# Three pairs of column groups of each feed-forward computed by Strassen's seven block products

## The chip, the cores and the metric

The kernel runs on one core of one Trainium2 chip. The metric is the device time of one execution in microseconds (us). A core has a matrix engine (TensorE; PE in the rows, its weight loads PEld), a vector engine (VectorE; DVE), a scalar engine (ScalarE; ACT), a general one (GpSimd; POOL) and a queue that issues transfers (SP). Each engine works through its own list of instructions in order, and semaphores hold an instruction until what it reads is there. TensorE writes into PSUM banks of 128 x 512 numbers; the other engines take the numbers from there to the on-chip buffer SBUF.

## The reference

256 tokens of width 1024 go through four layers, two of a first kind and two of a second. Each layer is a feed-forward, a mixer and another feed-forward, with norms between them. So there are eight feed-forwards, and all of them are

```
a, b = split(x @ w13, 2, axis=-1)      # x [256, 1024], w13 [1024, 2 x 2816]
(silu(a) * b) @ w2                     # w2 [2816, 1024]
```

In the second kind of layer x is the output of an RMS norm. Everything is float32.

## The kernel before

**Numbers.** TensorE multiplies in a format that keeps fewer bits than float32 (fp32r). Every operand is therefore split into a high part (a rounded copy, made by ScalarE) and a low part (operand minus high part, made by VectorE), and every product is made of three: high x high, high x low, low x high (`mm3`, L245).

**Weights.** They come as a stream of 712 units of 128 x 1024 numbers (512 KB). `fetch` (L197) loads a unit into one of four staging buffers `stg` through the SP queue; `split` (L205) makes `wh` (L215, ScalarE) and `wl` (L221, VectorE, a few on GpSimd) in two halves of 512 columns, so 4 instructions a unit. The split tiles lie in a ring of 48 buffers of 128 x 512, which is 12 units. A buffer is free again when the last matmul that reads it is done.

**Tokens.** The 256 tokens are two tiles of 128, each a generator (`tokens`). The second one lags by some units. The program is written in the order in which the generators are called; `split` is called some units ahead of the first tile (`lead`, L186). A scheduler then fixes the order on TensorE, ScalarE and VectorE at build time by priority and by what is ready and has a buffer; SP and GpSimd keep the order of the program.

**A feed-forward** (`ffn`, L324) has 11 groups of 256 columns of a and the same 256 of b.
- Groups 0 and 1: each tile by itself (`group`, L259), x as the stationary operand and 512 columns of weights streamed past it; then `hidden` and a transpose of the result (`transposed`, L230).
- Groups 2 to 10: both tiles together (`joint`, L363). The weights are stationary and the 256 tokens are streamed (L375), which gives the transposed result at once. A unit takes 24 matmuls of 256 columns; a group has four units. `gate` (L397) takes silu(a) b and splits it.
- Between the groups, `joint` multiplies what is finished with w2 (L387, by `mm3`), a unit of w2 at a time, with 12 matmuls of 512 columns for both tiles. The order is groups 2-3, 8 units of w2, groups 4-7, 8 units of w2, groups 8-10; the last 6 units of w2 each tile takes by itself (`rows`, L274).

Before a feed-forward the norm's result is transposed by TensorE and split into `xh` and `xl` (`to_x`, L251; ScalarE at L256, VectorE at L257).

Of the kernel before, what the change touches and what calls it, by code (L numbers as in the profile page):

```python
# [19 lines left out]
P = 128  # L20
# [10 lines left out]
# units by which the second token tile lags, and by which weights are split ahead; units in the  # L31
# ring of split weights, of which the last TAIL of a product are held longer; loads in flight
# [6 lines left out]
TAIL = 2  # L39
LAGS = dict(ffn=9, mixer1=6, mixer2=6)  # L40
# [3 lines left out]
# ticks between the steps of work that runs beside the products  # L44
# [23 lines left out]
class Core:  # L68
    """The two tiles of 128 tokens go through the network as two generators. Each yields after
    every unit of weights (one tick) it has multiplied with, or a number of ticks to be left  # L70
    alone; the second one lags, so that what lies between the products of one tile runs beside
    products of the other. Every engine issues in the order of this program."""

    def __init__(self, ctx, tc, a, out, order):
# [5 lines left out]
        self.whp = p("whp", 4 * RING)  # L80
# [5 lines left out]
        self.nunit = a["ws"].shape[0]  # L86
        self.phase = []
        for what, _ in order:
            for kind, n in (("ffn", 66), ("mixer1", 56) if what == "b1" else ("mixer2", 36), ("ffn", 66)):
                self.phase += [(kind, m) for m in range(n)]  # L90
# [30 lines left out]
    def start(self, g):  # L121
        """A generator of work beside the products; it yields ticks to wait."""
        done = {"done": False}

        def go():
            n = next(g, None)
            if n is None:
                done["done"] = True
            else:
                self.later(n, go)  # L130

        go()
        return done
# [5 lines left out]
    def run_all(self):  # L139
# [3 lines left out]
        def part(i, h):  # L143
            hi, lo = (t[:, i, 512 * h:512 * h + 512] for t in (self.xh, self.xl))
# [20 lines left out]
        while any(live):  # L165
# [20 lines left out]
    def lead(self):  # L186
        """Weights are split further ahead where the first tile is in a norm or the second one
        soon will be."""
        kind, n = self.phase[min(self.pos[0], self.nunit - 1)]
        left = dict(ffn=66, mixer1=56, mixer2=36)[kind] - n  # L190
        return LEAD + (MORE if n < FIRST else max(0, MORE - left // RAMP))

# [4 lines left out]
    def fetch(self, v):  # L197
        while self.next_dma <= min(v, self.nunit - 1):
            t = self.stg.tile([P, 1024], F32, tag="stg", name=self.nm("stg"))
            for c in (slice(0, 512), slice(512, 1024)) if self.next_dma == 0 else (slice(0, 1024),):  # L200
                self.nc.sync.dma_start(t[:, c], self.a["ws"][self.next_dma][:, c])
            self.stages[self.next_dma] = t
            self.next_dma += 1

    def split(self, u):  # L205
        while self.next_split <= min(u, self.nunit - 1):
            v = self.next_split
            self.fetch(v)
            w = self.stages.pop(v)
            wh, wl = [], []  # L210
            for h in range(2):
                half = w[:, h * 512:h * 512 + 512]
                wh.append(self.whp.tile([P, 512], F32R, tag="w", name=self.nm("wh")))
                wl.append(self.whp.tile([P, 512], F32R, tag="w", name=self.nm("wl")))
                r = self.nc.scalar.activation(wh[h], half, AF.Copy)  # L215
                if v < 3:
                    self.pin(r)
                if h and self.pool_share(*self.phase[v]):
                    self.nc.gpsimd.tensor_tensor(wl[h], half, wh[h], op=ALU.subtract)
                else:  # L220
                    self.nc.vector.tensor_sub(wl[h], half, wh[h])  # L221
            self.units[v] = (wh, wl)
# [13 lines left out]
    def to_T(self, src, name="xT"):  # L236
        """[tokens, 512] -> the two parts of its transpose [128, 4, tokens]."""
# [7 lines left out]
    def mm3(self, accs, xh, xl, wh, wl, start, stop):  # L245
        """accs[c] += x^T w[:, c] in the three products of parts that matter in float32."""
# [12 lines left out]
    def group(self, i, fn, extra=None):  # L259
        """A group of 512 columns, in units of two k-tiles."""  # L260
# [31 lines left out]

    def part(self, *xT):
# [5 lines left out]
    def row(self, src):  # L299
        """A row of 512, in every partition."""  # L300
# [8 lines left out]
    def prepare(self, i, n, *what):  # L309
        """Rows that both tiles use some time later, loaded once."""  # L310
# [1124 lines left out]
```

## Time and profile before

| | |
|---|---|
| time, median of 3 runs | 2220.77 us (2216.96 to 2222.27) |
| the profiled execution, from its first to its last instruction (span) | 2218.5 us |
| TensorE busy | 2184.9 us, 98% |
| VectorE busy | 1486.9 us, 67% |
| ScalarE busy | 1185.5 us, 53% |
| GpSimd busy | 282.5 us, 13% |
| mean transfer rate | 178 GB/s |

The page of the profile gives no other time of the profiled execution than its span; the median of the runs is 2.3 us more. Matmuls are pipelined, so their busy times overlap: what one costs is read from start to start, not from its duration.

### The profile page before, as it was taken

To read this page: it belongs to the slowest core of one execution; us is meant where nothing else is said; L and a number is where in the kernel's file an instruction comes from. 1 tells how busy PE (TensorE), PEld (TensorE's weight loads), DVE (VectorE), ACT (ScalarE), POOL (GpSimd) and SP (SyncE) were. 2 spreads that over 40 slices of the span, in tenths; PEclk is the share of its full clock that TensorE was granted. 3 is DMA by queue.
4 is the path that set the end of the run, shared out by engine and by line. 5 is a ranking of instruction groups with operands and counts; after the bars stand their busy time and mean duration, and the time that the engine had idled before them with its cause. 6 is when DMAs were issued, how large, how long until landed. Compare 5 with 4: busy or idle time off the path is not lost.

```text
span 2218.5 us, 35915 instructions
## 1 busy us (share of the span) xinstructions
PE 2184.9 (98%) x13440; PEld 1948.5 (88%) x13440; DVE 1486.9 (67%) x2553; ACT 1185.5 (53%) x2203; POOL 282.5 (13%) x319
## 2 busy tenths in 40 slices
PE   8999999999999999999999999999999999999998
PEld 7998888899899888889989997788998998788998
DVE  5656787655755779775585668776658566787463
ACT  5644755554544475554453554755446355576452
POOL 0000420000000033001001005610100100650000
PEclk9999999999999999999999999999999999999999
DMA  7854455655555445565545633527555464244561
GB/s 265 271 186 160 146 188 172 232 186 188 186 200 186 156 157 183 187 205 197 199 159 183 226 135 113 186 87 246 188 183 177 163 231 147 96 153 160 173 219 48
DMA packets 115327, 395.03 MB, mean 178 GB/s; under 512 B 12880, under 2 KB 15312, under 8 KB 115152
## 3 DMA queue, kind: packets, MB, share of 16 engines
q1 hardware_dynamic: 115152, 392.73, 52.1%
q8 instruction: 105, 1.72, 0.3%
q14 instruction: 70, 0.57, 0.1%
HBM read 391.63 MB, written 1.05 MB: 177 GB/s over the span
## 4 chain that ended last, share of the span: by engine, by line
PE 92%; DVE 4%; ACT 2%; DMA 1%; issue 1%; POOL 1%; SPq 0%; DVEq 0%; POOLq 0%; ACTq 0%
PE g L375 37%; PE big L249 27%; PE g L249 21%; PE g L233 2%; DMA stg<-in_ws_dram 1%; DVE wl L221 1%; PE big L1130 1%; PE big L660 1%; PE big L1159 1%; DVE qk L1001 1%; ACT wh L215 0%; PE big L1077 0%; PE big L862 0%; ACT xh L256 0%; PE big L1049 0%
## 5 line engine op out<-in xcount | busy, mean ns | idle before, releaser
L221 DVE TENSOR_TENSOR wl<-stg,wh 128x512 fp32r<-128x512 f32 x1410 | 966.1, 709 | 483.5 <-ACT wh L215 444.2
L215 ACT ACTIVATE wh<-stg 128x512 fp32r<-128x512 f32 x1424 | 846.9, 626 | 582.8 <-PE g L375 237.7
L375 PE MATMUL g<-xh,wh 128*128 128x256 f32 x2304 | 652.6, 283 | 0.0
L375 PE MATMUL g<-xl,wh 128*128 128x256 f32 x2304 | 652.0, 283 | 0.0
L375 PE MATMUL g<-xh,wl 128*128 128x256 f32 x2304 | 652.0, 283 | 0.0
L375 PEld LDWEIGHTS g<-xh,wl 128*128 128x128 f32 x2304 | 442.2, 192 | 0.9
L375 PEld LDWEIGHTS g<-xh,wh 128*128 128x128 f32 x2304 | 442.2, 192 | 0.9
L375 PEld LDWEIGHTS g<-xl,wh 128*128 128x128 f32 x2304 | 442.2, 192 | 0.0
L249 PE MATMUL g<-wh,xh 128*128 128x512 f32 x800 | 330.2, 413 | 11.2 <-ACT wh L215 6.7
L249 PE MATMUL g<-wl,xh 128*128 128x512 f32 x800 | 316.4, 396 | 0.0
L249 PE MATMUL g<-wh,xl 128*128 128x512 f32 x800 | 315.7, 397 | 0.5 <-DVE xl L257 0.3
L249 PEld LDWEIGHTS g<-wh,xh 128*128 128x128 f32 x800 | 152.8, 191 | 44.3 <-ACT wh L215 7.4
L249 PEld LDWEIGHTS g<-wh,xl 128*128 128x128 f32 x800 | 152.3, 190 | 36.8 <-DVE xl L257 3.9
L249 PE MATMUL big<-wh,hTh 128*128 128x512 f32 x576 | 182.8, 389 | 0.0
L249 PE MATMUL big<-wh,hTl 128*128 128x512 f32 x576 | 182.6, 389 | 0.0
L249 PE MATMUL big<-wl,hTh 128*128 128x512 f32 x576 | 182.6, 389 | 0.0
L249 PEld LDWEIGHTS g<-wl,xh 128*128 128x128 f32 x800 | 152.8, 191 | 27.6 <-DVE wl L221 0.4
L321 POOL TENSOR_TENSOR m<-m,nhalf 128x1 f32<-128x1 f32 (+1 forms) x24 | 23.1, 962 | 852.7 <-DVE m L320 852.7
L249 PEld LDWEIGHTS big<-wl,hTh 128*128 128x128 f32 x576 | 108.1, 188 | 22.6
L249 PEld LDWEIGHTS big<-wh,hTl 128*128 128x128 f32 x576 | 108.1, 188 | 22.5
L249 PEld LDWEIGHTS big<-wh,hTh 128*128 128x128 f32 x576 | 107.1, 188 | 21.3
L484 POOL TENSOR_TENSOR m<-m,nhalf 128x1 f32<-128x1 f32 x24 | 15.3, 638 | 646.6 <-DVE m L483 646.6
(297 smaller groups left out, 2158.9 us busy)
## 6 DMA issues: line engine op xcount, KB each, us to landing
stg<-in_ws_dram SPq DMA_DIRECT2D x711, 512.0 KB, 4.2
row<-in_norm_gain_dram SPq DMA_DIRECT2D x24, 256.0 KB, 5.6
row<-in_ln_g_dram SPq DMA_DIRECT2D x12, 256.0 KB, 4.8
row<-in_ln_b_dram SPq DMA_DIRECT2D x12, 256.0 KB, 6.3
xT<-in_xT_dram SPq DMA_DIRECT2D x4, 256.0 KB, 6.0
x<-in_x_dram SPq DMA_DIRECT2D x4, 256.0 KB, 6.9
out_dram<-x SPq DMA_DIRECT2D x4, 256.0 KB, 2.0
con<-in_con_dram SPq DMA_DIRECT2D x1, 528.0 KB, 6.9
```

Of the source, the lines that this page charges most:

```text
L215: r = self.nc.scalar.activation(wh[h], half, AF.Copy)
L221: self.nc.vector.tensor_sub(wl[h], half, wh[h])
L233: self.nc.tensor.transpose(tp[:, hs(j)], src[:, hs(j)], self.ident)
L249: self.nc.tensor.matmul(accs[c], a, b[c], start=start and q == 0, stop=stop and q == 2)
L321: self.nc.gpsimd.tensor_tensor(out, out, self.nhalf[:, 0:n], op=ALU.pow)
L375: nc.tensor.matmul(out, w[k // 4][:, hs(k % 4)], x[:, :, hs(k)], start=k + q == 0, stop=k == 7 and q == 2)
L484: self.nc.gpsimd.tensor_tensor(rs, rs, self.nhalf[:, 0:1], op=ALU.pow)
L660: nc.tensor.matmul(ps[:, 64 * h:64 * h + 64].rearrange("p (c m) -> p c m", m=m), Z[:, hs(h)], view(Z[:, hs(h)], m)[:, :, 1, :], start=True ...
L1001: eng.scalar_tensor_tensor(t[:, to], src[:, at], w(j), t[:, to], op0=ALU.mult, op1=ALU.add)
L1130: nc.tensor.matmul(ps[:, hh * S + j * P:hh * S + j * P + P], J["aq", i][r, hs(head // 2)], J["ak", j][r, hs(head // 2)], start=True, stop= ...
L1159: nc.tensor.matmul(o[:, 64 * hh:64 * hh + 64], pT[:, hs(2 * hh + j)], J["av", j][:, head * 64:head * 64 + 64], start=j == 0, stop=j == 1)
```

## The change

Of the nine groups that both tiles take together, six (2-3, 4-5, 6-7) are now done as three pairs. For a pair, x is a 2 x 2 matrix of blocks (two tiles of 128 tokens by two halves of 512 of the width; A11 to A22) and the weights are one too (two halves of the width by 512 columns of a and 512 of b; 11 to 22). Instead of eight block products, seven are made (`PRODUCTS`), each 128 tokens x 512 x 512 columns, as two units.

- `sums`: once a feed-forward, four sums of blocks of x (VectorE) and their splits. For that `to_x` keeps an unsplit copy of the transposed x where a feed-forward follows (`keep`).
- `operand`: the weight blocks are loaded unsplit into the ring (`raw`); four of the seven products need a sum of blocks, which VectorE makes, two units each, over 1024 columns.
- `split` of such a unit is one ScalarE and one VectorE instruction over 1024 columns instead of two of 512 each. The ring has the same size, but in 24 buffers of 128 x 1024, and now also holds the raw blocks and the sums.
- `pair`: the matmuls have x (or a sum) stationary and 512 columns of weights streamed. Several products add up in the same bank; ScalarE copies the intermediate states out of it (`keep`), VectorE adds them. The result lies by tokens and is transposed (`to_T`), 8 transposes of 128 x 128 a pair.
- The order is: pair 2-3, four units of w2, group 8, pair 4-5, four of w2, group 9, two of w2, pair 6-7, four of w2, group 10, two of w2; then the last six of w2. `lead` is 5 units where a pair is near.

Comments are also taken out. The number of loaded bytes is the same. Core of the diff:

```diff
+PAIR = 5
...
-BLOCKS = ((0, 4), (4, 8), (8, 11))
+FFN = (("s", 2), ("r", 0, 4), ("j", 8), ("s", 4), ("r", 4, 8), ("j", 9), ("r", 16, 18), ("s", 6),
+       ("r", 8, 12), ("j", 10), ("r", 18, 20))
+LAST = (12, 13, 14, 15, 20, 21)
+
+PRODUCTS = ("p1", "q5", "p6", "p3", "p7", "p2", "q4")
+NEEDS = dict(p1="11", q5="12", p6="22", p2="21")
...
-        self.whp = p("whp", 4 * RING)
+        self.whp = p("whp", 2 * RING)
...
-                self.split(min(self.pos[0] + self.lead(), self.next_split + STEP - 1))
+                self.split(min(self.pos[0] + self.lead(), self.next_split + STEP - 1 + self.paired()))
...
+        if self.made[min(self.pos[0] + PAIR, self.nunit - 1)]:
+            return PAIR
...
+    def operand(self, p, u):
+        raw, add = self.raw, self.nc.vector.tensor_add
+        if p == "p1":
+            return raw["11", u]
+        if p == "q5":
+            t = raw.pop(("11", u))
+            add(t, t, raw["12", u])
+            raw["t1", u] = t
+            return t
+        if p == "p6":
+            t = raw["t2", u] = self.whp.tile([P, 1024], F32, tag="w", name=self.nm("sum"))
+            add(t, raw.pop(("t1", u)), raw["22", u])
+            return t
+        if p == "p3":
+            return raw["22", u]
+        if p == "p7":
+            t = raw.pop(("12", u))
+            add(t, t, raw.pop(("22", u)))
+            return t
+        if p == "p2":
+            return raw["21", u]
+        t = raw.pop(("t2", u))
+        add(t, t, raw.pop(("21", u)))
+        return t
...
+            for h, c in enumerate(halves if made is None else [slice(0, 1024)]):
+                r = self.nc.scalar.activation(hi[:, c], w[:, c], AF.Copy)
...
+                    self.nc.vector.tensor_sub(lo[:, c], w[:, c], hi[:, c])
...
-    def to_x(self, i, srcs):
+    def to_x(self, i, srcs, keep=False):
...
+            if keep:
+                t = self.sh["A", i, h] = self.slot(name="A")
+                self.nc.scalar.activation(t, tp, AF.Copy)
...
+    def sums(self):
+        nc = self.nc
+        a11, a12, a21, a22 = (self.sh.pop(("A", i, h)) for i in range(2) for h in range(2))
+        nc.vector.tensor_sub(a22, a22, a21)
+        nc.vector.tensor_sub(a21, a11, a21)
+        nc.vector.scalar_tensor_tensor(a11, a22, -1.0, a11, op0=ALU.mult, op1=ALU.subtract)
+        nc.vector.scalar_tensor_tensor(a12, a11, -1.0, a12, op0=ALU.mult, op1=ALU.subtract)
+        X = {}
+        for p, t in (("q5", a22), ("p6", a11), ("p3", a12), ("p7", a21)):
+            hi, lo = self.slot((P, 512), F32R, "Xh"), self.slot((P, 512), F32R, "Xl")
+            nc.scalar.activation(hi, t, AF.Copy)
+            nc.vector.tensor_sub(lo, t, hi)
+            X[p] = hi, lo
+        for p, i, h in (("p1", 0, 0), ("p2", 0, 1), ("q4", 1, 1)):
+            X[p] = tuple(t[:, i, 512 * h:512 * h + 512] for t in (self.xh, self.xl))
+        return X
...
+    def pair(self, J, g):
+        nc = self.nc
+        bank, kept = {}, {}
+
+        def keep(p):
+            t = kept[p] = self.slot(name="k" + p)
+            nc.scalar.activation(t, bank[p], AF.Copy)
...
+        def hidden(i, t, sg):
+            nc.vector.scalar_tensor_tensor(t, t, -0.5 if J["rs", i] is None else -1.0, sg,
+                                           op0=ALU.mult, op1=ALU.mult)
+
+            def turn():
+                hi, lo = self.to_T(t, "hT")
+                for c in range(4):
+                    J["h", i, 2 * g + c] = hi[:, hs(c)], lo[:, hs(c)]
+
+            self.later(2, turn)
+
+        for p in PRODUCTS:
+            if p in ("p1", "q5", "p2"):
+                bank[p] = self.bank(self.grp, "g")
+            else:
+                bank[p] = bank["q5" if p == "p3" else "p1"]
+            xh, xl = J["X"][p]
+            for u in range(2):
                 wh, wl = self.units[self.pos[1]]
+                for j in range(2):
+                    k = 2 * u + j
+                    for q, (x, w) in enumerate(((xh, wh), (xh, wl), (xl, wh))):
+                        nc.tensor.matmul(bank[p], x[:, hs(k)], w[j], start=p in ("p1", "q5", "p2") and k + q == 0,
+                                         stop=k == 3 and q == 2, skip_group_check=True)
...
+                if u:
+                    if p in ("p1", "q5", "p6", "p7"):
+                        keep(p)
+                    if p == "p3":
+                        t = kept["p6"]
+                        nc.vector.tensor_add(t, t, bank[p])
+                    elif p == "p7":
+                        t = kept["p7"]
+                        nc.vector.tensor_add(t, t, kept.pop("q5"))
+                    elif p == "p2":
+                        t = kept.pop("p1")
+                        nc.vector.tensor_add(t, t, bank[p])
+                        silu(t, t, 0)
+                        hidden(0, kept.pop("p6"), t)
+                    elif p == "q4":
+                        t = self.slot(name="sg")
+                        silu(t, bank[p], 1)
+                        hidden(1, kept.pop("p7"), t)
                 yield
```

## Rows read from the trace of the kernel before

**Rows 1.** The page: busy time, share of the span, instructions; granted clock in 40 slices.
```profile
PE 2184.9 (98%) x13440; PEld 1948.5 (88%) x13440; DVE 1486.9 (67%) x2553; ACT 1185.5 (53%) x2203; POOL 282.5 (13%) x319
...
PEclk9999999999999999999999999999999999999999
```

**Rows 2.** The chain that ended last, in order of time: start, length, what.
```profile
60.02 21.79 PE big L249 x96
81.81 46.07 PE g L375 x384
...
211.30 19.06 PE g L249 x84
```

**Rows 3.** The same chain, transposes of one norm's result, 205 to 230 us.
```profile
210.43 0.87 PE g L233 x8
```

**Rows 4.** Busy time of each engine in the eight joint stages: last stage, then sum.
```profile
2047.50:2195.00 147.50, 147.50 (x1060) 139.97 (x1059) 79.01 (x124) 66.30 (x114) 0.00 (x0) 1.00 0.49 168
sum 1179.20, PE 1179.13 PEld 1118.38 DVE 679.72 ACT 586.28 POOL 34.74; mean PE 147.39 PEld 139.80 DVE 84.96 ACT 73.29 POOL 4.34
```

**Rows 5.** Groups by line, shapes apart: line, engine, operation, shapes | busy us, mean ns.
```profile
L411 DVE TENSOR_TENSOR hTl<-sg,hTh 128x512 fp32r<-128x512 f32 x72 | 49.8, 691 | 13.6 <-ACT hTh L410 9.7
...
L347 DVE TENSOR_TENSOR hT<-g,hT 128x256 fp32r<-128x256 f32 x32 | 13.4, 419 | 2.7 <-ACT hT L346 2.5
...
L256 ACT ACTIVATE xh<-g 128x512 fp32r<-128x512 f32 x44 | 23.8, 595 | 28.0 <-PE g L233 27.9
...
L346 ACT ACTIVATE hT<-g 128x256 fp32r<-128x256 f32 x32 | 12.1, 377 | 14.4 <-PE g L233 10.5 <-issue 3.6
```

**Rows 6.** Timeline of VectorE from 99 us.
```profile
99.16 3.17 DVE L221 TENSOR_TENSOR wl<-stg,wh 128x512 fp32r<-128x512 f32 x5
102.54 0.69 DVE L221 TENSOR_TENSOR wl<-stg,wh 128x512 fp32r<-128x512 f32 x1 [0.22 <-ACT wh L215]
103.98 0.69 DVE L221 TENSOR_TENSOR wl<-stg,wh 128x512 fp32r<-128x512 f32 x1 [0.75 <-ACT wh L215]
```

**Rows 7.** Timeline of ScalarE from 99 us.
```profile
99.46 1.14 ACT L215 ACTIVATE wh<-stg 128x512 fp32r<-128x512 f32 x2
...
103.32 0.63 ACT L215 ACTIVATE wh<-stg 128x512 fp32r<-128x512 f32 x1 [0.81 <-PE g L375]
```

**Rows 8.** Line 215 from 0 to 407.6 us, then from 0 to 596.8 us.
```profile
L215 ACT ACTIVATE wh<-stg x282: 612/631/659, 5.1 to 406.7; 128x512 fp32r<-128x512 f32 x141
...
L215 ACT ACTIVATE wh<-stg x415: 612/631/659, 5.1 to 596.5; 128x512 fp32r<-128x512 f32 x139
```

**Rows 9.** Waits, the longest in total: engine, line, releaser, us in total, times.
```profile
DVE wl L221 <- ACT wh L215: 444.2, 481, 4.8
ACT wh L215 <- PE g L375: 237.7, 310, 1.2
```

**Rows 10.** Busy time in the 24 us ahead of each joint stage: one, then sum.
```profile
573.00:597.00 24.00, 24.00 (x112) 19.56 (x113) 21.21 (x38) 15.17 (x29) 0.99 (x1) 1.00 0.53 182
...
sum 192.00, PE 188.01 PEld 152.66 DVE 167.58 ACT 131.81 POOL 10.82; mean PE 23.50 PEld 19.08 DVE 20.95 ACT 16.48 POOL 1.35
```

**Rows 11.** Timeline of VectorE, 570 to 583 us, first and last of 19 rows.
```profile
570.40 0.68 DVE L221 TENSOR_TENSOR wl<-stg,wh 128x512 fp32r<-128x512 f32 x1
...
582.18 0.42 DVE L347 TENSOR_TENSOR hT<-g,hT 128x256 fp32r<-128x256 f32 x1
```

**Rows 12.** Timeline of TensorE after one norm, 200 us.
```profile
200.41 1.03 PE L233 MATMUL g<-con,x 128*128 128x128 f32 x8
201.70 0.50 PE L249 MATMUL g<-wh,xh 128*128 128x512 f32 x1 [0.25 <-ACT xh L256]
```

**Rows 13.** Timeline of TensorE's first matmuls.
```profile
5.75 0.80 PE L249 MATMUL g<-wh,xh 128*128 128x512 f32 x1 [5.75 <-ACT wh L215]
...
7.49 0.63 PE L249 MATMUL g<-wh,xh 128*128 128x512 f32 x1
7.92 0.63 PE L249 MATMUL g<-wl,xh 128*128 128x512 f32 x1
```

More of the change, by code (lines that the diff above doesn't have):

```diff
@@ L85, in __init__ @@
         self.grp = p("grp", 4, space=PSUM)
[L86 to L87 removed]
+        self.phase, self.made = [], []
+        ffn = _ffn_units()
         for what, _ in order:
[L89 to L90 removed]
+            mixer = ("mixer1", 56) if what == "b1" else ("mixer2", 36)
+            for kind, made in (("ffn", ffn), (mixer[0], [None] * mixer[1]), ("ffn", ffn)):
+                self.phase += [(kind, m) for m in range(len(made))]
+                self.made += made
+        self.nunit = len(self.made)
+        self.raw, self.next_raw = {}, 0
         self.next_dma = self.next_split = 0
@@ L198, in fetch @@
         while self.next_dma <= min(v, self.nunit - 1):
[L199 to L202, printed above, removed]
-            self.next_dma += 1
+            made = self.made[self.next_dma]
+            if made is None:
+                t = self.stages[self.next_dma] = self.stg.tile([P, 1024], F32, tag="stg", name=self.nm("stg"))
+            elif made[0] in NEEDS:
+                t = self.raw[NEEDS[made[0]], made[1]] = self.whp.tile([P, 1024], F32, tag="w", name=self.nm("raw"))
+            else:
+                t = None
+            if t is not None:
+                for c in (slice(0, 512), slice(512, 1024)) if self.next_raw == 0 else (slice(0, 1024),):
+                    self.nc.sync.dma_start(t[:, c], self.a["ws"][self.next_raw][:, c])
+                self.next_raw += 1
+            self.next_dma += 1
+    def operand(self, p, u):
[22 more added lines that the diff above has]
+        return t
     def split(self, u):
@@ L208, in split @@
             self.fetch(v)
[L209 to L215, printed above, removed]
+            made = self.made[v]
+            w = self.stages.pop(v) if made is None else self.operand(*made)
+            hi = self.whp.tile([P, 1024], F32R, tag="w", name=self.nm("wh"))
+            lo = self.whp.tile([P, 1024], F32R, tag="w", name=self.nm("wl"))
+            halves = [slice(0, 512), slice(512, 1024)]
+            for h, c in enumerate(halves if made is None else [slice(0, 1024)]):
+                r = self.nc.scalar.activation(hi[:, c], w[:, c], AF.Copy)
                 if v < 3:
@@ L351, in hidden @@
             self.later(2, turn)
+        J["rs", i] = rs
+        if i == 1:
+            self.later(2, lambda: J.update(X=self.sums()))
         for g in range(OWN):
@@ L365, in joint @@
         nc = self.nc
-        for n, (g0, g1) in enumerate(BLOCKS):
-            for g in range(max(g0, OWN), g1):
+        for what, *at in FFN:
+            if what == "s":
+                yield from self.pair(J, *at)
+            elif what == "j":
                 acc = [self.bank(self.grp, "g") for _ in range(2)]
@@ L1334, in _rows, with _ffn_units, _blocks @@
     return w.reshape(-1, P, 1024)
-def _ffn(w_in, w_out):
-    w_in, w_out = np.concatenate([_pairs(w_in)[:4 * OWN], _chunks(w_in)[4 * OWN:]], 0), _rows(w_out)
-    return [w for a, b in BLOCKS for w in (w_in[4 * a:4 * b], w_out[2 * a:2 * b])]
+def _ffn_units():
+    out = [None] * (4 * OWN)
+    for what, *at in FFN:
+        if what == "s":
+            out += [(p, u) for p in PRODUCTS for u in range(2)]
+        else:
+            out += [None] * (4 if what == "j" else at[1] - at[0])
+    return out + [None] * len(LAST)
+def _blocks(w, g):
+    w = w.reshape(2, 512, 2, FF)[:, :, :, 256 * g:256 * g + 512]
+    parts = []
+    for p in PRODUCTS:
+        if p in NEEDS:
+            r, c = (int(n) - 1 for n in NEEDS[p])
+            parts.append(w[r, :, c].reshape(2, 2, P, 512).transpose(0, 2, 1, 3).reshape(2, P, 1024))
+    return np.concatenate(parts, 0)
+def _ffn(w_in, w_out):
+    own, chunks, w_out = _pairs(w_in)[:4 * OWN], _chunks(w_in), _rows(w_out)
+    parts = [own]
+    for what, *at in FFN:
+        if what == "s":
+            parts.append(_blocks(w_in, *at))
+        else:
+            parts.append(chunks[4 * at[0]:4 * at[0] + 4] if what == "j" else w_out[at[0]:at[1]])
+    return parts + [w_out[list(LAST)]]
 def _stream(v, order):
```

42 lines of the change are left out of this document (25 added, 17 removed).

## The prediction

> **What bounds the kernel now.** I read the page first: TensorE is busy 98% of the span, with the full granted clock in all 40 slices, VectorE 67%, ScalarE 53% [rows 1]. Then the chain that ended last, in order of time: the feed-forwards in it are unbroken runs of matmuls [rows 2]. Then the windows over the eight joint stages, the 147.4 us of each feed-forward in which both tiles go together: TensorE is busy 1179.13 of 1179.20 us, VectorE 679.72 (58%), ScalarE 586.28 (50%) [rows 4]. So here the time is the number of matmuls times their spacing, and VectorE and ScalarE have about 42% of it free. The change lives there: it takes from TensorE and gives to the other two.
>
> **TensorE, removed and added.** 384 matmuls of 256 columns (four groups) take 46.07 us: 120.0 ns each, 11.52 us a group, 23.04 us for the two groups that a pair replaces. A pair has 7 products x 12 = 84 matmuls of 512 columns; a run of just 84 of these takes 19.06 us. 96 in w2's part take 21.79 us: 2.72 us a unit [rows 2]. A pair adds 8 transposes, 0.87 us [rows 3]. So a pair saves 23.04 - 19.06 - 0.87 = 3.11 us, and the 24 pairs 74.6 us, if nothing else comes to decide. Of the 3.98 us ahead of the transposes, the product left out is worth 12 x 0.227 = 2.72; the other 1.26 come from wider matmuls.
>
> The Trainium skill (TensorE: Matmul & The Clock Gate, Back-to-back issue gap) gives N/2.4 + 2.5 ns, which is an estimate of 109.2 ns at 256 columns and 215.8 ns at 512, where the rows have 120.0 and 226.9. By it a pair would save 20.97 - 18.13 = 2.84 us instead of 3.98 ahead of the transposes, and the time would be 27 us later. The spacings of the trace decide.
>
> **VectorE, added.** No instruction of the trace has 1024 columns. 256 columns take 419 ns and 512 take 691 [rows 5], so 272 ns per 256; from start to start, 512 cost (3.17 - 0.69)/4 = 0.62 us [rows 6], and 1024 then cost 0.62 + 0.54 = 1.16. The bounds lie close: 1.08 (if the fixed part hides wholly) and 1.24 (two of 512). A pair has 14 low parts and 8 sums of blocks over 1024 columns (25.5 us), three adds, two products with silu and two low parts of the transpose over 512 (4.3 us): 29.9 us, where TensorE needs 19.9. Before, the two groups needed 16 low parts and four to six others, some 13 us. **Within a pair, VectorE is slower than TensorE by 10 us.** This is hidden only if it is done ahead, or made good in the units between the pairs.
>
> How far ahead can it be? At 407.6 us, where a joint stage begins, 282 high parts are done; TensorE has used up 130 units (66 + 56 + 8), 260 halves. So the splits are 11 units ahead, nearly the whole ring of 12; at 596.8 us it is 415 against 392 [rows 8]. In mid-stage ScalarE waits for TensorE to free a buffer (0.81 us each time, 237.7 us in all), and VectorE for ScalarE (444.2 us) [rows 6, 7, 9]: the ring's size, not the program's `lead`, sets how far ahead they run. The new ring holds 24 tiles of 1024 columns; 8 units split ahead (16 tiles) with 6 to 8 raw blocks or sums fit, so some 10 us of VectorE's work can be ahead of a pair.
>
> **The sum over the stretch that matters**, from the start of the first pair to the end of the third, with 10 units of w2 and two groups between them:
> - before, TensorE: 3 x 23.04 + 10 x 2.72 + 2 x 11.52 = 119.4 us;
> - after, TensorE: 3 x 19.06 + 2 x 0.87 + 50.2 = 109.2 us;
> - after, VectorE: 3 x 29.9 + 18 ordinary units x 1.24 + some 3.1 for the two gates = 115.1 us. Ahead of it lie 11 units x 1.24 = 13.6 us, as before, less 8 instructions of `sums` (5.0 us) that come new into the stage ahead: 8.6 us. Left: 106.5 us.
>
> The two engines are level: 106.5 us of VectorE's work in 109.2 of TensorE's. So what VectorE loses to waits decides. Bounds: between 570.40 and 582.60 us it has 19 rows of work without an idle time (1.0) [rows 11]; over the eight 24 us ahead of the joint stages, where it also races to fill the ring, it is busy 167.58 of 192 us (0.873) [rows 10]. I take the middle, 0.937: 106.5/0.937 = 113.7 us, a gain of 119.4 - 113.7 = 5.7 us for each feed-forward. What would be late next are TensorE's matmuls on low parts. VectorE's own waits are the adds that wait for a product in PSUM: behind such an add stand the next low parts, for which TensorE waits.
>
> **ScalarE.** Two of 512 start 0.51 us apart [rows 7]; the width adds (595 - 377) = 0.22 us per 256 [rows 5], so 1024 cost 0.95 us. A pair: 14 x 0.95 + 8 copies and silus of 512 (0.51) = 17.4 us of 19.9. It stays below VectorE, but a high part that comes late is one of the waits in the 0.937. The copy out of p1's bank must be done before p6 adds to it; q5 lies between, 2.72 us.
>
> **Smaller parts.** The third pair's transposes fall after the stretch: 0.87 us. `to_x` with its unsplit copy puts one more ScalarE copy (595 ns) ahead of the high part for which TensorE already waits 0.25 us after a norm [rows 5, 12]: 0.6 us at 7 of the 8 feed-forwards (not the first, where x comes from memory) for one tile, nothing for the other, whose norm lies beside matmuls; both exposed would be twice that. 4.2 us in all, 0 to 8.4. Transfers: the same bytes; 8 raw blocks in 19.9 us instead of 23. Before, the copies wait for buffers, not for transfers, so I put nothing down; if a raw block waits for a place in the ring, this is the second rival below.
>
> **Time.** Each feed-forward: 5.7 - 0.87 - 0.53 = 4.3 us, times 8 = 34.4. 2218.5 - 34.4 = 2184.1 us of span, and with the 2.3 us by which the median of the runs is above it: **2186 us**, 1.6% faster. A difference within 0.3% (6.7 us) is about what a measurement of this kernel cannot tell from no change.
>
> **Rivals.**
> - *TensorE stays the bound throughout* (VectorE keeps over 0.975): 8 x (10.2 - 1.4) = 70 us, 2150 us. For it: the 11 units ahead, and the stretch without idle times. Against it: a buffer of ten microseconds between two engines that are equally loaded seldom hides everything.
> - *VectorE decides, and it is slower.* Place: the pairs. It decides from 0.903 on (106.5/0.903 = 118.0 us, where the gain is gone). At 0.873, the lower row, the stretch takes 122.0 us: 8 x (2.6 + 1.4) = 32 us more, 2253 us. For it: in-order engines that wait for each other twice a unit (the sum before the high part, the high part before the low). Against it: the sums wait for nothing but a transfer and can go between.
> - *The ring does not hold the work ahead*, because raw blocks and sums lie in it from the load on: if only three units of a pair are done ahead (4.6 us), each pair takes 25.3 us, the stretch 126.1, and 8 x (6.7 + 1.4) = 65 us are lost: 2286 us. Against it: the count of 24 tiles above.
> - *Nothing measurable*: VectorE near 0.90 to 0.915, 2214 to 2227 us.
> - *The granted clock falls.* Now it is full in every slice [rows 1]. What half of it costs is seen only in the first matmuls, after 5.75 us without one: they start 0.43 us apart [rows 13] where later ones take 0.227, though the clock's row does not show that start. If waits in a pair made the clock fall to 1.2 GHz for one product of seven, 2.72 us x 24 = 65 us would be lost against my forecast: 2251 us. The Trainium skill (TensorE: Matmul & The Clock Gate, Why this matters for your kernels) states that pauses of TensorE between bursts bring the clock down to half; no row of before has such a pause in a joint stage, so the trace neither bears it out nor denies it.
>
> **Chances.** Forecast (2157 to 2213): 0.48. TensorE the bound throughout: 0.13. Nothing measurable: 0.10. VectorE decides: 0.20. Ring: 0.06. Clock: 0.03. Faster by over 0.3%: 0.61; within: 0.10; slower: 0.29. The range reaches from just under the full gain, 2143, to the lower row of VectorE, 2253; it leaves out the ring's case and half of the worse ones. The forecast's own range is 2157 to 2213.
>
> **What would show it.** In the profile of the changed kernel: 84 matmuls of a pair in 19.1 us where no wait is among them; VectorE instructions of 1024 columns at some 1.23 us; VectorE over 90% busy from the first pair to the third's end; TensorE's idle time there ended by VectorE's low parts, most of it in the second half of a pair and in the first pair; the stretch 113.7 us long against 119.4. I am wrong if VectorE has idle time in a pair while TensorE waits too (then order or the ring is the cause), if TensorE waits for copies out of the banks, or if the time between feed-forwards grows by more than 1 us each.

## The result and the profile after

The changed kernel takes **2272.7 us** (median of 4 runs, 2271.39 to 2275.31) against 2219.94 us before on the same chip (2216.96 to 2222.27; with a fourth run, the median is 0.8 us lower than that of the first three). The ratio is 1.0241, with a 95% interval of 1.0226 to 1.0255: it is slower by 2.4%, where 1.6% faster was forecast, and it lies 60 us above the forecast's own range (2157 to 2213) and 20 us above the wide one (to 2253). The profiled execution has a span of 2273.5 us, 55.0 more than before.

The page, busy time of each engine (answers to [rows 1]):

```profile
PE 2146.6 (94%) x11040; PEld 1802.6 (79%) x11040; DVE 1894.3 (83%) x2809; ACT 1355.8 (60%) x2311; POOL 273.0 (12%) x319
```

TensorE is busy 38 us less, though part of its busy time is now at half clock (below), and it is idle for 127 us where it was idle for 34. VectorE has 407 us more. So the question is where TensorE stands still. First the windows over the stretch of the prediction, from the start of the first pair to the end of the third (one of the eight, then the sum; the columns are window and length, busy time of PE, PEld, DVE, ACT and POOL, granted clock, DMA share, GB/s):

```profile
423.60:535.80 112.20, 110.29 (x584) 94.28 (x583) 103.41 (x123) 74.04 (x109) 0.00 (x0) 1.00 0.57 210
...
sum 905.40, PE 889.58 PEld 756.64 DVE 823.87 ACT 575.02 POOL 34.64; mean PE 111.20 PEld 94.58 DVE 102.98 ACT 71.88 POOL 4.33
```

The mean stretch is 905.40/8 = 113.2 us, forecast was 113.7, and by the prediction's sum the same work took 119.4 before. TensorE is busy 98% of it. **The stretch gained 8 x 6.2 = 50 us, where 46 were predicted; the loss is elsewhere.** The windows over its three pairs:

```profile
423.60:442.80 19.20, 19.20 (x86) 15.67 (x85) 18.91 (x24) 14.94 (x24) 0.00 (x0) 1.00 0.65 230
466.60:485.40 18.80, 18.80 (x85) 15.54 (x84) 18.80 (x22) 14.39 (x22) 0.00 (x0) 1.00 0.48 171
516.80:535.60 18.80, 18.80 (x85) 15.57 (x84) 18.23 (x23) 14.71 (x22) 0.00 (x0) 1.00 0.62 219
```

Each of these pairs takes the 19 us of its matmuls (18.8 to 20.3 in feed-forwards two to eight, 20.6 to 22.6 in the first), TensorE without a gap, and VectorE is full too (18.91 of 19.20, 18.80 of 18.80). Now the stage ahead, in which each tile takes groups 0 and 1 by itself ("own stage" from here on). Windows of the kernel before over this stage of the second feed-forward:

```profile
384.00:407.60 23.60, 23.60 (x110) 19.41 (x111) 21.20 (x39) 16.48 (x30) 1.00 (x1) 1.00 0.56 194
```

The same stage after, then the sum over all eight feed-forwards:

```profile
389.00:423.60 34.60, 25.98 (x108) 20.49 (x108) 27.47 (x39) 13.94 (x21) 1.00 (x1) 0.85 0.06 19
...
sum 268.30, PE 197.92 PEld 156.07 DVE 220.11 ACT 125.67 POOL 12.80; mean PE 24.74 PEld 19.51 DVE 27.51 ACT 15.71 POOL 1.60
```

**The own stage grew from 23.6 to 34.6 us, and the granted clock fell to 0.85.** The first feed-forward's stage is 26.7 us of the sum; the other seven, at 23.7 before (23.6 and 23.8 in two of them), cost 268.3 - 26.7 - 165.9 = 75.7 us more. With the stretches, -49.8 + 75.7 = +25.9 of the 55.0 us. The transposes of the third pair are 8 x 0.87 = 7.0 of the rest, the norms some 7 (below); about 15 us were not followed up. The timeline of TensorE in this stage (start, length, instruction, idle time ahead and what ended it):

```profile
388.02 0.50 PE L302 MATMUL g<-wh,xh 128*128 128x512 f32 x1 [1.27 <-ACT xh L312]
...
415.02 0.66 PE L286 MATMUL g<-con,sg 128*128 128x128 f32 x2 [8.59 <-DVE sg L413]
...
416.34 0.63 PE L302 MATMUL g<-wh,xl 128*128 128x512 f32 x1
416.76 0.63 PE L302 MATMUL g<-wh,xh 128*128 128x512 f32 x1
...
420.82 0.40 PE L302 MATMUL g<-wh,xh 128*128 128x512 f32 x1
421.06 0.39 PE L302 MATMUL g<-wl,xh 128*128 128x512 f32 x1
```

TensorE stands still for 8.59 us, ahead of the transposes of the first tile's result for group 1, until VectorE has made silu(a) b (`sg`, L413). (The 48 matmuls of the first tile's two groups have all started by 400.22 us. The expectations below call this gate the second tile's; by the order of the program it is this one of the first, and the second tile's follow.) Then 11 matmuls of 512 columns (from 415.34 to 420.18 us) start 0.43 us apart, and only then 0.23: the lower level of the clock, 1.2 GHz (granted clock 0.50 from 415.02 to 420.59 us), costs some 11 x 0.2 = 2.2 us. 8.6 + 2.2 = 10.8 of the 11.0 us by which this stage grew. What VectorE did meanwhile, in its timeline:

```profile
400.40 0.69 DVE L313 TENSOR_TENSOR xl<-g,xh 128x512 fp32r<-128x512 f32 x1 [0.71 <-ACT xh L312]
401.01 0.68 DVE L354 TENSOR_TENSOR A<-A,A 128x512 f32<-128x512 f32 x1
...
402.21 1.22 DVE L274 TENSOR_TENSOR wl<-raw,wh 128x1024 fp32r<-128x1024 f32 x1
403.34 0.69 DVE L355 TENSOR_TENSOR A<-A,A 128x512 f32<-128x512 f32 x1
403.94 1.22 DVE L239 TENSOR_TENSOR raw<-raw,raw 128x1024 f32<-128x1024 f32 x1
...
407.95 1.22 DVE L244 TENSOR_TENSOR sum<-raw,raw 128x1024 f32<-128x1024 f32 x1
...
412.12 1.22 DVE L250 TENSOR_TENSOR raw<-raw,raw 128x1024 f32<-128x1024 f32 x1
413.25 1.29 DVE L362 TENSOR_TENSOR Xl<-A,Xh 128x512 fp32r<-128x512 f32 x2
414.46 0.42 DVE L413 SCALAR_TENSOR_TENSOR sg<-g,sg 128x256 f32<-128x256 f32 x1
```

From 400.40 to 414.46 us VectorE has no idle time and does almost nothing but work for the first pair: `sums` (L354 to L362), sums of weight blocks (L239, L244, L250) and low parts (L274). The gate of 0.42 us stands behind all of it. But VectorE's queue holds it up only at the end. The gate reads silu(a), which ScalarE makes (L411) from matmuls that were done at 400.6 us, and in ScalarE's timeline this silu comes only now:

```profile
409.29 1.06 ACT L268 ACTIVATE wh<-sum 128x1024 fp32r<-128x1024 f32 x1 [2.97 <-DVE sum L244]
410.25 1.65 ACT L361 ACTIVATE Xh<-A 128x512 fp32r<-128x512 f32 x3
411.81 0.36 ACT L411 ACTIVATE sg<-g 128x256 f32<-128x256 f32 x1
```

From 401.73 us on there stand ahead of it three high parts of weight blocks and four of the sums of x, and one of the high parts waits 2.97 us for VectorE's sum. The silu is done at 412.17 us, and only from there to 414.46 us does the gate stand behind VectorE's own order alone. So the pair's work is ahead of the group's result in two queues; which of them alone would suffice for the wait was not tried.

The waits of TensorE, the longest in total (us, times, longest):

```profile
PE g L286 <- DVE sg L413: 27.7, 4, 8.6
PE g L563 <- DVE m L694: 26.7, 3, 8.9
PE g L286 <- DVE kp L487: 13.3, 15, 1.4
PE g L302 <- ACT xh L312: 10.7, 13, 1.3
PE g L286 <- DVE sg L416: 7.9, 2, 7.1
```

The first two and the last are this one wait in the different kinds of layers (where x comes from a norm that left the tokens' factors out, it falls on L563, which spreads these factors); with two small ones on L563 (3.7 and 1.8) they make **67.8 us**, called "own waits" below. Before, TensorE waited 3.1 us in all for the gates of these groups.

### The profile page after: what moved, and what is told of

Read it like the earlier page. It is cut to its first block, busy times and chain, and to the rows that moved or that the text cites. A ratio compares the mean times of both kernels' runs of the same rounds, so it can differ in the third digit from the quotient of the medians.

```text
span 2273.5 us, 30712 instructions
## 1 busy us (share of the span) xinstructions
PE 2146.6 (94%) x11040; PEld 1802.6 (79%) x11040; DVE 1894.3 (83%) x2809; ACT 1355.8 (60%) x2311; POOL 273.0 (12%) x319
## 4 chain that ended last, share of the span: by engine, by line
PE 62%; DVE 19%; DMA 7%; ACT 6%; issue 5%; POOL 1%; SPq 0%; DVEq 0%; ACTq 0%; POOLq 0%
PE g L302 19%; PE big L302 18%; PE g L508 11%; DVE wl L274 9%; PE g L454 8%; DMA stg<-in_ws_dram 4%; ACT wh L268 4%; DMA raw<-in_ws_dram 3%; PE g L286 3%; DVE sum L244 1%; DVE sum L255 1%; PE big L1270 1%; DVE Xl L362 1%; DVE raw L250 1%; PE big L1299 1%
## 5 line engine op out<-in xcount | busy, mean ns | idle before, releaser
L274 DVE TENSOR_TENSOR wl<-stg,wh 128x512 fp32r<-128x512 f32 x1026 | 698.4, 719 | 168.2 <-ACT wh L268 159.8
L268 ACT ACTIVATE wh<-stg 128x512 fp32r<-128x512 f32 x1040 | 597.0, 623 | 292.7 <-DMA stg<-in_ws_dram 143.6
L268 ACT ACTIVATE wh<-raw 128x1024 fp32r<-128x1024 f32 x240 | 248.1, 1056 | 106.4 <-DVE raw L239 59.1
L274 DVE TENSOR_TENSOR wl<-raw,wh 128x1024 fp32r<-128x1024 f32 x240 | 287.8, 1220 | 19.8 <-ACT wh L268 16.7
L454 PE MATMUL g<-xl,wh 128*128 128x256 f32 x768 | 217.3, 283 | 0.0
L454 PE MATMUL g<-xh,wl 128*128 128x256 f32 x768 | 217.3, 283 | 0.0
L454 PE MATMUL g<-xh,wh 128*128 128x256 f32 x768 | 217.2, 283 | 0.0
L302 PEld LDWEIGHTS g<-wh,xh 128*128 128x128 f32 x800 | 156.9, 196 | 53.5 <-ACT xh L312 14.8
L508 PE MATMUL g<-wl,Xh 128*128 128x512 f32 x384 | 149.9, 390 | 0.8 <-DVE wl L274 0.8
L508 PE MATMUL g<-wh,Xh 128*128 128x512 f32 x384 | 149.7, 390 | 0.0
L508 PE MATMUL g<-wh,Xl 128*128 128x512 f32 x384 | 149.5, 389 | 0.0
L454 PEld LDWEIGHTS g<-xh,wl 128*128 128x128 f32 x768 | 147.4, 192 | 0.9
L454 PEld LDWEIGHTS g<-xh,wh 128*128 128x128 f32 x768 | 147.3, 192 | 0.9
```

The lines of the kernel that those rows point to most:

```text
L268: r = self.nc.scalar.activation(hi[:, c], w[:, c], AF.Copy)
L274: self.nc.vector.tensor_sub(lo[:, c], w[:, c], hi[:, c])
L302: self.nc.tensor.matmul(accs[c], a, b[c], start=start and q == 0, stop=stop and q == 2)
L454: nc.tensor.matmul(out, w[k // 4][:, hs(k % 4)], x[:, :, hs(k)], start=k + q == 0, stop=k == 7 and q == 2)
L508: nc.tensor.matmul(bank[p], x[:, hs(k)], w[j], start=p in ("p1", "q5", "p2") and k + q == 0, stop=k == 3 and q == 2, skip_group_check=True)
```

## The experiments

Times are medians, and each ratio is to the kernel before on the same chip; its medians lie between 2218.2 and 2220.1 us.

**One: less work ahead.** `lead` near a pair from 5 units to 2.

```diff
-PAIR = 5
+PAIR = 2
```

> One number is changed: the lead near a pair is 2 units instead of 5, so fewer units of the first pair are split ahead of the second tile's own gates in the program. Theory 1 (order of the queues): the 8.6 us wait of TensorE in the stage in which each tile goes by itself, and the slow clock behind it (some 2.4 us), come from low parts and sums of the pair that stand ahead of that tile's own gate (or its factor) in VectorE's and ScalarE's queues. With some 9 us of them behind instead, the wait falls to 2 to 4 us and the time to some 2205 to 2230 us. Theory 2 (too much work for VectorE, in whatever order): what TensorE no longer waits for there, it waits for in the first pair; 2265 to 2280 us.

2254.13 us, 1.0161 [1.0144, 1.0177], between the two expectations. The wait on L413 falls from 8.6 to 5.1 us at its longest, the own waits from 67.8 to 42.0 us (L561 18.0, L413 14.8, L416 9.2), but the second and third pair of the second feed-forward now take 21.1 and 22.0 us. The wait is caused by work for the pair, and what is taken from there is missing in the pairs.

**Two: the sums of x later**, by six ticks (calls of the two tiles' generators), so that they fall behind the own groups.

```diff
-            self.later(2, lambda: J.update(X=self.sums()))
+            self.later(8, lambda: J.update(X=self.sums()))
```

> Only the sums of x's blocks (8 VectorE and 4 ScalarE instructions, 5 us of VectorE) are put into the program 6 ticks later, behind the second tile's own gates. Theory 1: the wait in the own stage loses these 5 us, falls to some 3.6 us, some of it comes back as a wait of the second product for its sum of x; 2215 to 2235 us. Theory 2: 2265 to 2280 us, with the wait moved into the first pair.

2238.28 us, 1.0086 [1.0070, 1.0103]: 34 us back, 4.3 for each feed-forward, where `sums` is 5.0 us of VectorE's time; it is 3 us above the first expectation. The own waits are still 39.1 us. In the second feed-forward the wait is 4.5 us and now lies behind the first product of the first pair, which takes 26.6 us with the lower clock after it.

**Three: a plain group between the own stage and the first pair**, with the sums of x early (three) or late too (four). Group 8 goes first, and groups 9 and 10 ahead of the other pairs.

```diff
-FFN = (("s", 2), ("r", 0, 4), ("j", 8), ("s", 4), ("r", 4, 8), ("j", 9), ("r", 16, 18), ("s", 6),
-       ("r", 8, 12), ("j", 10), ("r", 18, 20))
+FFN = (("j", 8), ("s", 2), ("r", 0, 4), ("j", 9), ("s", 4), ("r", 4, 8), ("r", 16, 18), ("j", 10), ("s", 6),
+       ("r", 8, 12), ("r", 18, 20))
```

> The same work in another order: group 8 comes before the first pair (then pair, four units of w2, group 9, pair, six units of w2, group 10, pair, six units of w2). TensorE has 11.5 us there in which VectorE is asked for 6.6. The sums of x still come early. Theory 1: the pair's low parts are no longer ahead of the own gates, only the sums are; the wait falls to 2 to 4 us; 2200 to 2225 us. Theory 2: only the 4.9 us that VectorE has free beside the group are won of some 11 in each feed-forward; 2230 to 2240 us.

> Group 8 before the first pair, and the sums of x 6 ticks later as well, so that they run beside group 8. Theory 1: neither sums nor the pair's low parts are ahead of the own gates, and the wait is gone: the stretch gain of 6 us is kept in each feed-forward; 2165 to 2195 us, faster than the kernel before. Theory 2: as with the group first alone, 2230 to 2240 us.

Three: 2244.54 us, 1.0118 [1.0094, 1.0141], above both expectations, with own waits of 26.0 us. Four: **2220.59 us, 1.0008 [0.9999, 1.0018]**, between its two expectations: 52 us less than the changed kernel and no different from the kernel before. The own waits are 8.3 us. What now remains is in part VectorE in the pairs: in the second feed-forward they take 18.9, 23.2 and 20.5 us. The second pair takes 23.1 to 23.2 us in feed-forwards two to four, 18.8 to 18.9 in the last four. TensorE also waits 10.6 us in all for a last VectorE instruction of the norms (L597), 2.1 in the changed kernel. The windows of experiment four over the 23.5 us ahead of the second pair and over this pair:

```profile
440.00:463.50 23.50, 23.50 (x154) 21.36 (x153) 16.64 (x21) 9.93 (x15) 0.00 (x0) 1.00 0.59 226
463.50:486.70 23.20, 20.95 (x88) 15.74 (x87) 20.39 (x22) 14.89 (x20) 0.00 (x0) 1.00 0.37 136
```

VectorE idles 6.9 us just ahead of the pair in which it is late. In that time ScalarE waits in order for a product; its timeline:

```profile
457.98 0.60 ACT L542 ACTIVATE sg<-g 128x512 f32<-128x512 f32 x1 [4.80 <-PE g L454]
```

**Five: four without the eight sums of weight blocks of a pair**, which are 29 us of VectorE's time for each feed-forward. The core (likewise for the other products):

```diff
         if p == "q5":
-            t = raw.pop(("11", u))
-            add(t, t, raw["12", u])
-            raw["t1", u] = t
-            return t
+            return raw["12", u]
```

> The kernel with group 8 first and the late sums of x, and without the eight VectorE instructions a pair that add weight blocks: products take single blocks instead, so the output is another one. VectorE has 8 x 1.14 = 9.1 us less in each pair, 219 us in all. Theory A (what is left of the loss is VectorE's load: the second pair of that kernel lasts 23 us instead of 19, and TensorE waits for the norm's last VectorE instructions): the waits go, the joint stage falls to some 139 us against 147.6; 2150 to 2170 us. Theory B (the loss is latency of the chain sum, high part, low part, or the copies out of the banks, and the other parts of the change): 2200 to 2215 us.

2178.50 us, 0.9812 [0.9795, 0.9828]: 42 us less than with the sums, though 8 to 28 us above the expectation. The edit takes away more than VectorE's time: ScalarE's wait for each sum and the buffers of the new sums go too, so theory A is not told apart from the chain's latency. The page:

```profile
PE 2117.9 (97%) x11040; PEld 1791.1 (82%) x11040; DVE 1678.9 (77%) x2617; ACT 1349.3 (62%) x2311; POOL 274.0 (13%) x319
```

**Six: four, with the sums for p7 and q4 on GpSimd**, which has little to do in the joint stages [rows 4].

```diff
+        if p in ("p7", "q4"):
+            add = lambda o, a, b: self.nc.gpsimd.tensor_tensor(o, a, b, op=ALU.add)
```

> The kernel with group 8 first and late sums, with four of the eight weight sums of a pair (those of the products p7 and q4) on GpSimd, which is idle in the joint stage. VectorE has 4.6 us less in each pair; GpSimd needs some 3 us for each of these sums (1443 to 1689 ns for 512 columns before). Theory A (VectorE's load): half of the way to the kernel without weight sums, 2180 to 2200 us. Rival: GpSimd's sums come late or slow VectorE down beside them; 2215 to 2240 us.

2356.05 us, 1.0610 [1.0594, 1.0626]: slower by 135 us than four and far above both expectations. Groups by line, VectorE's low parts of raw blocks, first in the changed kernel (1219 ns in four):

```profile
L274 DVE TENSOR_TENSOR wl<-raw,wh 128x1024 fp32r<-128x1024 f32 x240 | 287.8, 1220 | 19.8 <-ACT wh L268 16.7
```

and in experiment six:

```profile
L276 DVE TENSOR_TENSOR wl<-raw,wh 128x1024 fp32r<-128x1024 f32 x240 | 394.3, 1669 | 32.4 <-ACT wh L270 30.7
```

Groups of GpSimd there, one of its two kinds of sums:

```profile
L236 POOL TENSOR_TENSOR raw<-raw,raw 128x1024 f32<-128x1024 f32 x48 | 135.1, 2816 | 520.3 <-DVE raw L241 179.7 <-DMA raw<-in_ws_dram 178.1 <-DVE wl L276 94.2
```

VectorE has 96 instructions less and is busy longer (1956.9 us against 1888.5 in four). One place in the timeline of GpSimd, experiment six:

```profile
443.74 2.40 POOL L236 TENSOR_TENSOR sum<-sum,raw 128x1024 f32<-128x1024 f32 x1 [14.15 <-DMA raw<-in_ws_dram]
446.96 2.52 POOL L236 TENSOR_TENSOR sum<-sum,raw 128x1024 f32<-128x1024 f32 x1 [0.81 <-DMA raw<-in_ws_dram]
```

and the same place in VectorE's:

```profile
443.94 6.62 DVE L276 TENSOR_TENSOR wl<-raw,wh 128x1024 fp32r<-128x1024 f32 x2
```

Two low parts that otherwise take 2.4 us take 6.6 beside two adds on GpSimd of 2.4 and 2.5 us: 4.2 of GpSimd's 4.9 us are lost to VectorE. The Trainium skill (SBUF — State Buffer, Who interferes with whom) states that a VectorE instruction with two inputs in SBUF contends with a GpSimd instruction that reads SBUF, and calls such contention an exclusive lock; the 6.62 us agree. How the 135 us divide between this and sums that come late was not measured.

**Seven: four with two pairs**; groups 4 and 5 go as plain groups.

```diff
-... ("j", 9), ("s", 4), ("r", 4, 8), ("r", 16, 18), ("j", 10), ...
+... ("j", 9), ("j", 4), ("r", 16, 18), ("j", 5), ("r", 4, 8), ("j", 10), ...
```

> The kernel with group 8 first and late sums, with two pairs instead of three: groups 4 and 5 are done by the weights-stationary way again, between the two pairs. TensorE's gain is 2 x 3.1 - 0.5 = 5.7 us a feed-forward instead of 8.8, and VectorE has 17 us less to do in each. Theory A (VectorE's load): no wait is left, 2170 to 2185 us, faster than three pairs. Theory B (latency and other parts): each pair still costs some waits, 2205 to 2220 us.

**2193.61 us, 0.9879 [0.9864, 0.9894]**: the fastest full version, 1.2% faster than the kernel before and 79 us faster than the changed one, though 8 us above the first expectation. Both pairs take 18.8 us. Its page:

```profile
PE 2142.8 (98%) x11840; PEld 1843.6 (84%) x11840; DVE 1753.5 (80%) x2745; ACT 1297.5 (59%) x2295; POOL 273.3 (12%) x319
```

**Eight: seven, with the unsplit copy in `to_x` behind the high part.**

```diff
+            self.nc.scalar.activation(hi, tp, AF.Copy)
             if keep:
                 t = self.sh["A", i, h] = self.slot(name="A")
                 self.nc.scalar.activation(t, tp, AF.Copy)
-            self.nc.scalar.activation(hi, tp, AF.Copy)
```

> The kernel with two pairs, with the unsplit copy of the transposed x made behind the high part instead of ahead of it. If the copy's place is what makes TensorE wait 0.74 to 1.11 us for the high part after a norm (0.25 us before), 0.5 us come back for the first half at 14 norms, up to 7 us: 2186 to 2191 us. If the wait is hidden or moves to the low part, no change: 2192 to 2195 us.

2196.20 us, 0.9896 [0.9881, 0.9911], against 0.9879 in seven: nothing gained. After one norm (at 565 us in seven, 563 us here) TensorE's wait for the high part goes from 1.11 to 0.62 us, and a wait of 0.39 us for the low part appears behind it.

**Nine: the changed kernel's start with two pairs** (its order, lead and early sums; group 4 and 5 plain). If the load of the later pairs made the wait, it would shrink.

```diff
-FFN = (("s", 2), ("r", 0, 4), ("j", 8), ("s", 4), ("r", 4, 8), ("j", 9), ("r", 16, 18), ("s", 6),
+FFN = (("s", 2), ("r", 0, 4), ("j", 8), ("j", 4), ("r", 16, 18), ("j", 5), ("r", 4, 8), ("j", 9), ("s", 6),
```

> The changed kernel with its own start (a pair first, sums of x early, lead 5), but two pairs instead of three. If the wait in the own stage comes from the order of the queues there and nothing else, it stays whole (8.6 us and the slow clock at each feed-forward) although VectorE has 17 us less to do in each: the 52 us that lie between the changed kernel and the one with group 8 first and late sums come on top of 2193.6: some 2245 us. If it comes from VectorE's load over the feed-forward, it shrinks with the load: 2195 to 2215 us.

2281.38 us, 1.0275 [1.0257, 1.0292], 36 us above the first expectation. The timeline of TensorE:

```profile
412.49 0.66 PE L286 MATMUL g<-con,sg 128*128 128x128 f32 x2 [8.58 <-DVE sg L413]
```

The wait is the same to 0.01 us, and the own waits are 68.1 us against 67.8. It does not depend on how many pairs follow: it is made in the own stage, by work for the first pair. The kernel is even 9 us slower than with three pairs: in the changed kernel the second pair took 18.8 us, fewer than two plain groups (23.0).

**Ten: the edits of one and two together**, in the changed kernel's order: nothing of the first pair's work is forced ahead of the gate. If the order on VectorE alone were the cause, the loss would go.

> The changed kernel in its own order (a pair first, three pairs) with both edits that each helped: lead 2 and the sums of x 6 ticks later. If the order in the own stage is the whole loss there, both together take the wait away and the time comes to that of the kernel with group 8 first, some 2215 to 2225 us. If the pair's work must be done somewhere before its matmuls, TensorE waits in the first pair instead of the own stage, and the time stays between: 2230 to 2245 us, hardly below the kernel with late sums alone (2238.3).

2271.61 us, 1.0237 [1.0219, 1.0256]: 1 us gained, and above both expectations. The waits of TensorE:

```profile
PE g L508 <- ACT wh L268: 26.1, 30, 1.2
PE g L508 <- DVE wl L274: 21.9, 28, 2.1
```

The longest wait on L413 is now 1.6 us and the own waits are 13.0 us in all, but the pairs, whose line is L508, wait 48 us for their operands and take 23.4, 27.0 and 19.7 us in the second feed-forward. This order only moves the wait.

**Eleven: the new ring and code without any pair**, in the order of the kernel before, without the sums of x and the unsplit copies.

```diff
-FFN = (("s", 2), ("r", 0, 4), ("j", 8), ("s", 4), ...
+FFN = (("j", 2), ("j", 3), ("r", 0, 8), ("j", 4), ("j", 5), ("j", 6), ("j", 7), ("r", 8, 16),
+       ("j", 8), ("j", 9), ("j", 10))
```

> The changed kernel with no pair: groups 2 to 10 by the weights-stationary way in the order of the kernel before, no sums of x, no unsplit copies of x. What stays of the change is the ring in 24 tiles of 1024 columns. If that ring (a unit's two halves share a tile) costs something by itself, the time is above 2225 us; if not, it is that of the kernel before, 2217 to 2223 us.

2216.93 us, 0.9995 [0.9986, 1.0004]: 24 buffers of 1024 columns cost nothing by themselves, that is without raw blocks and sums in them.

**Twelve: the changed kernel without the sums of weight blocks** (edit of five, everything else as changed).

> The changed kernel in its own order, lead and early sums of x, without the eight VectorE instructions a pair that add weight blocks (products take single blocks, so the output is another one). In the changed kernel's trace five of these sums (5.7 us) stand on VectorE between the second tile's norm and its own gate, ahead of which TensorE waits 8.6 us. If the wait there is work that VectorE must do ahead of the first pair, it falls to some 3 us and the time to 2200 to 2225 us. If it is the place of the gate in the queue alone, whatever stands before it, the wait stays above 6 us and the time above 2245 us.

2233.04 us, 1.0062 [1.0045, 1.0079], 40 us less than the changed kernel and between the two expectations. The timeline of TensorE (this kernel is 12 lines shorter: L274 and L401 are L286 and L413 of the changed one):

```profile
402.70 0.66 PE L274 MATMUL g<-con,sg 128*128 128x128 f32 x2 [4.39 <-DVE sg L401]
```

The own waits fall from 67.8 to 39.5 us. With four, five and the changed kernel this is a square:

| | with the sums of weight blocks | without |
|---|---|---|
| order of the changed kernel, sums of x early | 2272.7 | 2233.0 |
| a plain group first, sums of x late | 2220.6 | 2178.5 |

The order with a plain group first and late sums of x is worth 52 and 55 us, leaving out the sums of weights 40 and 42. Each holds with or without the other: the two add up, 94 us in all.

## Why the prediction was wrong

**Right.** The terms of TensorE (19.06 us a pair; 18.8 to 19.2 measured without a wait), of VectorE (an estimated 1.08 to 1.24 us for 1024 columns; 1.13 from start to start, 402.21 to 403.34) and the stretch itself, 113.7 forecast and 113.2 measured. The last is in part luck, for two misses cancel in it: VectorE was busy 103.0 us there and not 106.5, and 0.910 of the time (823.87 of 905.40) and not 0.937.

**The step that failed** is the term "Ahead of it lie 11 units x 1.24 = 13.6 us, as before, less 8 instructions of `sums` (5.0 us) that come new into the stage ahead: 8.6 us", which was set down as free. It was counted as a stock that VectorE brings along; for the stage where this stock is made the sum had no term at all, which puts TensorE's wait there at nothing without a reason. VectorE was busy 87% of the 24 us ahead of each joint stage already [rows 10], and now it had to put the sums of x and the first pair's low parts and weight sums there, ahead of a gate of 0.42 us that TensorE's next instruction needs; ScalarE had their high parts ahead of the silu for this gate. That cost 8.6 us of waiting and 2.2 us through half clock behind it: 10.8 us, against the 6.2 us that the stretch gained. The stage grew from 23.6 to 34.6 us. Two and twelve show the two kinds of this work: the sums of x put later give 34 us back, the weight sums left out 40, though twelve leaves them out of all three pairs and not of the first alone. Nine shows that the wait does not depend on how many pairs follow.

The stretch came out right partly for that reason: VectorE could keep up in it because TensorE had waited ahead of it. Ten, which takes the stock away, has pairs of 23.4 and 27.0 us. **The sum had to begin at the start of the own stage.** There VectorE has 27.5 + 103.0 = 130.5 us of work, and TensorE 23.6 + 109.2 = 132.8, where before it had 23.6 + 119.4 = 143.0. To break even VectorE must be busy 130.5/143.0 = 0.913 of the time from the norm to the third pair's end, and the 0.937 that was taken for the stretch leaves 143.0 - 139.3 = 3.7 us ahead of the smaller parts, not 5.7. So the amount of work alone, counted from there, would still have given a gain: it explains 2.0 us of the miss. The other 8.5 us (147.8 measured instead of 139.3) come from the share of the time in which VectorE worked: the changed order reaches only 130.5/(34.6 + 113.2) = 0.88. That the place of the work is behind most of this, four shows: with another order and later sums of x it gets 52/8 = 6.5 us back in each feed-forward and comes out level with the kernel before.

**The rivals.** "VectorE decides" had the right engine and a time (2253) 20 us short, at the wrong place: it was priced in the pairs, and the wait came where VectorE runs ahead for them. "The clock falls" came true at that place too: 2.2 us for a feed-forward, behind the wait, and nothing in the pairs (granted clock 1.00 in all three). The Trainium skill (TensorE: Matmul & The Clock Gate, Why this matters for your kernels) states that pauses between bursts bring the clock down to half; after the pause of 8.59 us the spacing of 0.43 us agrees. "The ring does not hold the work ahead" (the third in the list, which the prediction once calls the second) had the nearest time, 2286 us, by luck: it put 25.3 us on each pair, and they took 18.8 to 20.3 us in feed-forwards two to eight. In the wait ahead of them VectorE had no idle time from 400.40 us on, so no buffer or transfer held it there. Eleven says only that the size of the buffers costs nothing. In "Nothing measurable" the shares do not fit the times: by the prediction's own sum, 0.90 to 0.915 gives some 2223 to 2208 us.

**The signs.** VectorE was over 90% busy in the stretch, as said. But TensorE's waits there were not for low parts (3.3 us in all for those of the pairs), and none of the signs for being wrong names the own stage, which grew by 11.0 us; the nearest to it is the time between feed-forwards.

**Smaller parts.** `to_x` was put at 0.6 us of wait per norm for one tile; TensorE's first matmul behind the norm shown waits 1.27 us instead of 0.25 [rows 12], 1.0 more. Eight shows that this is not the copy's place in ScalarE's order alone. The transposes of a pair's result wait for VectorE (13.3 us on L487 in all), which the sum put at nothing.

**Open.** Five is 28 us above the 2150 us of TensorE's terms alone, and seven 8 us above what was expected; where these lie was not followed, and neither were about 15 of the 55 us of the changed kernel. Whether a schedule exists in which three pairs are faster than two is open: order, lead and the time of the sums were tried, but not a silu and a gate that go ahead of the pair's work on ScalarE and VectorE.

## What to carry to other kernels

Work that is said to be done ahead has to be paid for in the stage where it is done: begin the sum at the point from which the helping engine runs ahead, not where its work is used, and look there, in the queue of every helping engine, for the small instructions that the main engine needs and that will stand behind the new work (here a silu of 0.36 us on ScalarE and a gate of 0.42 us on VectorE). If an order that removes one wait only moves it (ten), the engine has too much to do at that place; if giving the stage room brings the time back (three, four), the place was wrong; here both held, and doing the change at two places out of three (seven) beat doing it everywhere. Half clock after a wait belongs in the price of the wait: 2.2 us on 8.6 here.

## What the runs showed of the hardware

- Adds on GpSimd did not relieve VectorE in this kernel: with 1024 columns they took 2.8 us, and VectorE's own instructions of 1024 columns that make the low parts of raw blocks went from 1219 to 1669 ns on average (four and six).
- A wait of 8.6 us was followed by 5.6 us at the lower clock (0.50 granted from 415.02 to 420.59 us): 11 matmuls 0.43 us apart, then 0.23. Over the whole span the granted clock is 0.978, where the kernel before has 0.995 to 0.998.
